# A hybrid mLSTM and SSD layer on one core: scalar and vector work queued behind the products' evacuations, with earlier first loads and other buffers for small rows

## The chip, the cores and the metric

The kernel runs on one core of one Trainium2 chip. The metric is the device time of one launch in microseconds; the time before is the median of three runs. A core has five engines with an instruction stream each, all in order: PE multiplies matrices into PSUM, DVE (vector) and ACT (scalar) read PSUM and SBUF, POOL works on SBUF, and SP issues the DMAs here. An instruction that waits holds up whatever stands behind it on its engine.

## The reference, cut to what matters

```python
h = rms_norm(x, norm_w)
proj = h @ w_in                                   # 2048 x 1024 times 1024 x 6680
q, k, v, i_pre, f_pre, o_pre, z_m, z_s, xbc, dt_raw = split(proj)
hm = mlstm_chunkwise(q, k, v, log_i, log_f)       # 4 heads, chunks of 128 tokens
hm = rms(hm) * mlstm_norm_w * sigmoid(o_pre) * silu(z_m)
xs, Bm, Cm = split(silu(causal_conv4(xbc)))
y = ssd_chunked(xs, dt, A, Bm, Cm) + d_skip * xs  # 2 groups of 8 heads, chunks of 128
y = grouped_rms(y * silu(z_s)) * ssd_norm_w
out = rms_norm(x + concat(hm, y) @ w_out, final_norm_w)
```

## The kernel before, in words

The sequence of 2048 tokens is worked in two halves (`s` = 0 and 1) and two output stages. Each of these four stages is a row of jobs: 26 jobs for each half (a pair of 128-column blocks of the input projection: for each head `h0` to `h3` four pairs, for each group `g0`, `g1` five) and eight jobs for each half of the output projection. A job is one Strassen product of 2x2 blocks with seven block products, each 12 matmuls of 128x128 by 128x512 (every operand is split into a high and a low part, three matmuls for each of four blocks). They all have line L270; the tile names tell the product: R11, R21, T2, T3, T1, R22, T4 are the right operands, L11, L12, S2, S3, S1, S4, L22 the left ones.

The seven right operands stay in SBUF for a stage. During the last job of a stage each is loaded anew for the next one (`refill`, L390, two 1 MB DMAs for each operand, high and low part). The left operands are made for each job from two weight (or mix) tiles by `left_sums` and `split` (L191 on ACT, L192 on DVE).

`strassen` accumulates four of the products in one PSUM tile `pa`, and copies an intermediate sum out after each: L276 after R11, L283 after T2, L289 after T1, and `copy` (L302 or L327) after R22. The next product into `pa` must wait for that copy. DVE adds two other tiles in (L280, L290, L296). Jobs overlap by two products, so that PE's order is T2, T3 of job n, R11 of job n+1, T1 of n, R21 of n+1, R22 of n, T4 of n. Between T1 and R22 stands only one other product.

After each product the function `step` runs. It first makes one piece of left operand (`left`), issues a refill if one is due, and then traces background work: gate computations and chunks that are due after so many steps (`tick`, `later`), generators planned for this step (`plan`), and one piece of the recurrence of the head or group whose projections were finished last (`wv.to`, class `Weave`). The background generators that matter here:

- `rec_head`: for each of eight chunks `load` (L676 `hin`, L678 the rows `nmi`), `scores` (L686 to L704: row mask on DVE, exponentials `E` L688 and `w` L690 on ACT, then matmuls L694), `memory` (L714 to L735), and later `turn`.
- `rec_group`: `load` (L788 `gin`), `decay` (L795 `E` loaded and made an exponential), `tokens` (matmuls L813, L814, L817), `states` (L841: four scalings of `y` on ACT), `update`, `outs`, and later `norm` (L889) and `spread` (L901).
- `next_h` and `next_w`: the right operands of the second half and of the output stages, made in the background and stored to DRAM. `next_w` loads four pieces of `w_out` (L532), scales them on ACT (L533), and `sums_out` forms the seven operands; each goes through two tiles of tag `hq` (three buffers), a high part made on ACT (L396) and a low part on DVE (L398), both stored by L537.

PE keeps the order in which the program is traced. On the other engines a planner sets the order when the program is built: among the instructions that its own model takes to be ready it places the first, so that background work can stand on ACT or DVE ahead of an evacuation that was traced before it. Buffers come from tags with a fixed number of slots; an instruction that needs a slot waits until the tile before has been used up.

Of the kernel before, what the change touches and what calls it, by code (L numbers as in the profile page):

```python
# [69 lines left out]
def hybrid_layer(ctx, tc, x, norm_w, w_in, b_igate, b_fgate, conv_w, conv_b, dt_bias,  # L70
# [35 lines left out]
    def r1(nm, n=NV):  # L106
        return mk([P, 272], "r1", 6, nm)[:, 0:n]

    def r5(nm, n=P):
        return mk([P, n], "r5", 9, nm)  # L110

# [153 lines left out]
    def product(ps, L, R, start):  # L265
        lh, ll = L
        rh, rl = R
        for k in range(4):
            for n, (l, r) in enumerate(((lh, rh), (lh, rl), (ll, rh))):
                nc.tensor.matmul(ps, lhsT=l[:, k, :], rhs=r[:, k, :], start=start and k + n == 0,  # L270
                                 stop=k == 3 and n == 2, skip_group_check=True)

    def strassen(L, R, oa, ob, copy):
        pa = pj_tile()
        product(pa, L["L11"], R["R11"], True)
        nc.scalar.copy(oa[0], pa)  # L276
        yield
        ps = pj_tile()
        product(ps, L["L12"], R["R21"], True)
        nc.vector.tensor_add(oa[0], ps, oa[0])  # L280
        yield
        product(pa, L["S2"], R["T2"], False)
        nc.scalar.copy(ob[0], pa)  # L283
        yield
        pd = pj_tile()
        product(pd, L["S3"], R["T3"], True)
        yield
        product(pa, L["S1"], R["T1"], False)
        nc.scalar.copy(ob[1], pa)  # L289
        nc.vector.tensor_add(ob[1], pd, ob[1])  # L290
        yield
        product(pa, L["S4"], R["R22"], False)
        copy(oa[1], pa)
        yield
        product(pd, L["L22"], R["T4"], False)
        nc.vector.tensor_add(ob[0], pd, ob[0])  # L296

# [3 lines left out]
    def evac_copy(dst, ps):  # L301
        nc.scalar.copy(dst, ps)  # L302

    def pair(L, R, s, ph, kind, j):
# [20 lines left out]
        if kind == "oz":  # L325
            def first(dst, ps):
                nc.scalar.activation(dst, ps, AF.Tanh, scale=0.5)  # L327

# [191 lines left out]
    def next_w():  # L520

        for j in range(2):
            for k in range(4):
                e = mk([P, HPG, P], "e4", 1, "we").rearrange("p a b -> p (a b)")
                q = {(0, 0): e[:, 0:TB], (1, 0): e[:, TB:]}
                for b in range(2):
                    q[b, 1] = mk([P, 6, P], "g3", 2, "wg").rearrange("p a b -> p (a b)")[:, 0:TB]
                for a in range(2):
                    r = j * 8 + a * 4 + k
                    for b in range(2):  # L530
                        u = q[a, b]
                        nc.sync.dma_start(u, w_out[r * P:(r + 1) * P, b * TB:(b + 1) * TB])  # L532
                        nc.scalar.activation(u, u, AF.Copy, scale=nwo[:, r:r + 1])  # L533
                yield

                def dst(o, i, v):
                    nc.sync.dma_start(wsd[j][o][:, i, k, :], v)  # L537

                yield from sums_out(q, dst)
# [128 lines left out]
    def rec_head(s, h):  # L668
# [3 lines left out]
        def load(n):  # L672
            b, c = seq[n]
            o = (b % 2) * TB + c * P
            t = r2("hin").rearrange("p (a l) -> p a l", a=4)
            nc.sync.dma_start(t, hd[s][h][:, 0:4, o:o + P])  # L676
            nmi = r2("nmi", 2 * P).rearrange("p (a l) -> p a l", a=2)
            nc.sync.dma_start(nmi, mrowd[b][:, h, c * P:(c + 1) * P].partition_broadcast(P))  # L678
            L["in", n] = (t, nmi)
# [27 lines left out]
        def memory(n):  # L707
# [11 lines left out]
            if C is None:  # L719
                C = S["C"] = mk([P, NV + 14], "C", 1, "C")[:, 0:NV]  # L720
                nc.vector.tensor_copy(C, cps[:, 0:NV])
# [8 lines left out]
            sq = mk([P, 1], "sq", 3, "sq")  # L730
            nc.scalar.activation(mk([P, DV], "r5", 9, "sj", BF16), nps[:, 0:DV], AF.Square, accum_out=sq)  # L731
            nc.scalar.copy(mx, nps[:, 0:DV])
# [21 lines left out]

        load(0)
        S["C"] = None
        if s:
            C = S["C"] = mk([P, NV + 14], "C", 1, "C")[:, 0:NV]
            nc.sync.dma_start(C, cd[h])
# [17 lines left out]
    def rec_group(s, g):  # L777
# [127 lines left out]
        load(0)  # L905
        decay(0)
        S["H"] = None
        if s:
# [25 lines left out]

    NREC = {"h": 10, "g": 25}

    class Weave:
# [3 lines left out]
        def set(self, g, n, total):  # L941
            self.finish()
            self.g, self.n, self.done, self.i, self.total = g, n, 1, 0, total
            next(g)
# [60 lines left out]
    def step(n, o):  # L1005

        left()
        if n + 1 < len(jobs) and jobs[n + 1]["new"]:
            st = jobs[n + 1]["stage"]
            Rs[st][o] = refill(o, refs[st])  # L1010
        tick()
        for t in [k for k in plan if k <= clock[0]]:
# [21 lines left out]
    for n, jb in enumerate(jobs):  # L1034
# [35 lines left out]
        if more:  # L1070
            next(jobs[n + 1]["gen"])
            step(n + 1, "R21")
        next(g)
        step(n, "R22")
        next(g)
        step(n, "T4")
        next(g, None)
        if "s" in jb and (n + 1 == len(jobs) or jobs[n + 1].get("ph") != jb["ph"]):
            nxt = [k for k in jobs[n + 1:] if k.get("ph") == jobs[n + 1].get("ph") and k["stage"] == jobs[n + 1]["stage"]]
            wv.set(rec(jb["s"], jb["ph"]), NREC[jb["ph"][0]], 7 * len(nxt) if "s" in jobs[n + 1] else 42)  # L1080
            if jb["ph"] == "h1":
                bgq = next_w() if jb["s"] else next_h()
                total = 64 if jb["s"] else 84
                for i in range(total):
# [31 lines left out]
```

## Time and profile before

| what | value |
|---|---|
| time, median of 3 runs (lowest to highest) | 1823.45 us (1819.24 to 1826.52) |
| time of the profiled execution | 1829.99 us |
| its span, first to last instruction | 1828.2 us |
| PE busy, weight load | 1679.5 us (92%), 1357.2 us (74%) |
| DVE, ACT, POOL busy | 1308.7 us (72%), 880.6 us (48%), 450.2 us (25%) |
| DMA moved, mean rate | 405.32 MB, 222 GB/s |
| mean granted TensorE clock | 0.966 of full speed |

PE is busy nearly all the time, so the span is PE's work, plus the stretches in which PE waits, plus what a lowered clock adds. Busy shares of the other engines do not bound the time by themselves; what counts is which of them PE waits for, and what stood ahead of the awaited instruction on its engine.

### The profile page before, as it was taken

The page shows a single profiled execution, that of the slowest core. Times are in us where ns is not written, and L with a number is a line of the kernel's source. Part 1 is how long each engine was busy: PE and PEld are TensorE (multiplying, and loading weights), DVE is VectorE, ACT ScalarE, POOL GpSimd, SP SyncE. Part 2 cuts the span into 40 slices and gives each one's busy share as a digit, 9 for nine tenths or more (in the row PEclk, how much of TensorE's full clock was granted, in tenths as well). Part 3 has the DMA queues.
Part 4 walks back from the last instruction along what each step waited for, and adds up shares of the span by engine and source line. Part 5 has one row for each costly group of instructions (what it writes and reads, how often), then busy time and mean ns, then how long its engine had stood idle before and what let it go on. Part 6 is the DMA issues. An engine that isn't in the chain of part 4 may idle for free.

```text
span 1828.2 us, 25057 instructions
## 1 busy us (share of the span) xinstructions
PE 1679.5 (92%) x8072; PEld 1357.2 (74%) x8072; DVE 1308.7 (72%) x2417; ACT 880.6 (48%) x1880; POOL 450.2 (25%) x629
## 2 busy tenths in 40 slices
PE   4999999999899798989899999898988889997997
PEld 4688887778788685767788777777776667776885
DVE  7677968877567693888675895655678578864775
ACT  5344644456566663434564444655565433332443
POOL 2000413332122131223121331202211144532222
PEclk9999999999999899999999999999999989998999
DMA  5245666668787689655575658888877976678543
GB/s 153 93 156 174 185 212 203 207 212 256 224 258 231 181 274 379 206 182 179 161 203 185 196 181 272 290 278 263 258 260 250 384 260 212 205 265 315 189 158 115
DMA packets 358323, 405.32 MB, mean 222 GB/s; under 512 B 30224, under 2 KB 284432, under 8 KB 352816
## 3 DMA queue, kind: packets, MB, share of 16 engines
q1 hardware_dynamic: 358192, 403.72, 68.1%
q8 instruction: 64, 1.05, 0.2%
q14 instruction: 67, 0.55, 0.1%
HBM read 251.40 MB, written 152.24 MB: 221 GB/s over the span
## 4 chain that ended last, share of the span: by engine, by line
PE 25%; DMA 15%; DVE 7%; issue 3%; ACT 2%; SPq 1%; POOL 1%; DVEq 0%; POOLq 0%; ACTq 0%
PE pj L270 21%; DMA E<-arow 1%; DMA we<-in_w_out 1%; DVE E L798 1%; DMA nmi<-mrow 1%; DMA mx<-mix 1%; DMA gin<-gd 1%; DMA ws1R<-hqh 1%; DMA T4l<-ws1T 1%; DMA ws0T<-hql 1%; DMA ws0R<-hqh 1%; DMA ws0T<-hqh 1%; DMA xr<-in_x 1%; DMA ws1T<-hqh 1%; PE rc L872 1%
## 5 line engine op out<-in xcount | busy, mean ns | idle before, releaser
L733 POOL TENSOR_SCALAR sq<-dn,sq 128x1 f32<-128x1 f32 x64 | 46.1, 720 | 624.9 <-ACT sj L731 477.8
L270 PE MATMUL pj<-R22h,S4h 128*128 128x512 f32 x272 | 119.7, 440 | 38.1 <-ACT ob L289 24.6
L270 PE MATMUL pj<-T2h,S2h 128*128 128x512 f32 x272 | 113.4, 417 | 11.6 <-ACT ca L276 9.3
L270 PE MATMUL pj<-T1l,S1h 128*128 128x512 f32 x272 | 107.3, 395 | 7.6 <-DMA T1l<-ws1T 7.2
L270 PE MATMUL pj<-R22l,S4h 128*128 128x512 f32 x272 | 113.1, 416 | 0.0
L270 PE MATMUL pj<-T4h,L22h 128*128 128x512 f32 x272 | 111.5, 410 | 1.4 <-DMA T4h<-ws1T 1.4
L270 PE MATMUL pj<-R11h,L11h 128*128 128x512 f32 x272 | 112.7, 414 | 0.0
L270 PE MATMUL pj<-R22h,S4l 128*128 128x512 f32 x272 | 112.7, 414 | 0.0
L270 PE MATMUL pj<-T2l,S2h 128*128 128x512 f32 x272 | 109.0, 401 | 4.0 <-DMA T2l<-hsT 3.3
L270 PE MATMUL pj<-T1h,S1h 128*128 128x512 f32 x272 | 111.0, 408 | 1.4 <-ACT cbt L283 1.4
L270 PE MATMUL pj<-R21h,L12h 128*128 128x512 f32 x272 | 110.1, 405 | 0.0
L270 PE MATMUL pj<-T3h,S3h 128*128 128x512 f32 x272 | 109.3, 402 | 0.0
L270 PE MATMUL pj<-T2h,S2l 128*128 128x512 f32 x272 | 108.6, 399 | 0.0
L270 PE MATMUL pj<-T1h,S1l 128*128 128x512 f32 x272 | 107.2, 394 | 1.3 <-DVE S1l L192 1.3
L270 PE MATMUL pj<-T4l,L22h 128*128 128x512 f32 x272 | 106.6, 392 | 1.9 <-DMA T4l<-ws1T 1.9
L270 PE MATMUL pj<-T4h,L22l 128*128 128x512 f32 x272 | 106.7, 392 | 0.0
L270 PE MATMUL pj<-R11h,L11l 128*128 128x512 f32 x272 | 106.6, 392 | 0.0
L270 PE MATMUL pj<-R11l,L11h 128*128 128x512 f32 x272 | 106.5, 391 | 0.0
L270 PE MATMUL pj<-T3h,S3l 128*128 128x512 f32 x272 | 106.3, 391 | 0.0
L270 PE MATMUL pj<-R21l,L12h 128*128 128x512 f32 x272 | 106.3, 391 | 0.0
L270 PE MATMUL pj<-R21h,L12l 128*128 128x512 f32 x272 | 106.3, 391 | 0.0
L270 PE MATMUL pj<-T3l,S3h 128*128 128x512 f32 x272 | 106.3, 391 | 0.0
(330 smaller groups left out, 4697.4 us busy)
## 6 DMA issues: line engine op xcount, KB each, us to landing
wa<-in_w_in SPq DMA_DIRECT2D x52, 512.0 KB, 6.2
s<-sum SPq DMA_DIRECT2D x52, 512.0 KB, 5.3
hd<-ob SPq DMA_DIRECT2D x32, 512.0 KB, 3.8
E<-arow SPq DMA_DIRECT2D x32, 512.0 KB, 5.2
hin<-hd SPq DMA_DIRECT2D x64, 256.0 KB, 4.7
mx<-mix SPq DMA_DIRECT2D x32, 512.0 KB, 4.9
wb<-in_w_in SPq DMA_DIRECT2D x26, 512.0 KB, 4.2
sum<-ls SPq DMA_DIRECT2D x26, 512.0 KB, 4.6
```

Source lines behind the costliest of these rows:

```text
L270: nc.tensor.matmul(ps, lhsT=l[:, k, :], rhs=r[:, k, :], start=start and k + n == 0, stop=k == 3 and n == 2, skip_group_check=True)
L733: nc.gpsimd.tensor_scalar(sq, dn, DV * EPS, sq, op0=ALU.mult, op1=ALU.add)
L798: nc.vector.tensor_scalar(E[:, r, :], E[:, r, :], G["cum"][:, c, k:k + 1], 0.0, op0=ALU.subtract, op1=ALU.min)
L872: nc.tensor.matmul(yps[o:o + HD, (r // 2) * P:(r // 2 + 1) * P], lhsT=xdt[:, r * HD:(r + 1) * HD], rhs=E[:, r, :], start=True, stop=True, ...
```

## The change

Four edits are made together.

1. Every evacuating instruction of `strassen` is recorded (`tie`): the last one on ACT under "a", the last on DVE under "v". In `step` all background work (`tick`, `plan`, `wv.to`, now in `behind`) is traced inside `tc.issue_after` of both: what it puts on ACT is placed behind the last recorded ACT instruction, what it puts on DVE behind the last DVE one. `left` and `refill`, the work at a job's end (tanh, convolution, stores) and the queues of POOL and SP are not tied.
2. The first piece of a recurrence (`load(0)`, and `decay(0)` for a group) is traced two products earlier, before R22 of the last job of its phase. A yield is added behind it, so the weave counts 11 pieces for a head and 26 for a group, of which two are done when it starts.
3. `next_w` loads its four pieces, yields three times, and only then scales them. Its pieces rise from 64 to 80 over the same 76 steps.
4. Buffers: the rows `nmi` move from tag `r2` (7 slots of 512 columns) to `r1`, which grows from 6 to 8 slots of 272 columns; `r5` shrinks from 9 to 8 slots of 128; the head state `C` takes the single slot of the group state `H`.

```diff
-        return mk([P, 272], "r1", 6, nm)[:, 0:n]
+        return mk([P, 272], "r1", 8, nm)[:, 0:n]
-        return mk([P, n], "r5", 9, nm)
+        return mk([P, n], "r5", 8, nm)
...
+    tied = {}
+
+    def tie(k, i):
+        tied[k] = i.ins
+
     def strassen(L, R, oa, ob, copy):
         pa = pj_tile()
         product(pa, L["L11"], R["R11"], True)
-        nc.scalar.copy(oa[0], pa)
+        tie("a", nc.scalar.copy(oa[0], pa))
...
-        nc.vector.tensor_add(oa[0], ps, oa[0])
+        tie("v", nc.vector.tensor_add(oa[0], ps, oa[0]))
...
         product(pa, L["S1"], R["T1"], False)
-        nc.scalar.copy(ob[1], pa)
-        nc.vector.tensor_add(ob[1], pd, ob[1])
+        tie("a", nc.scalar.copy(ob[1], pa))
+        tie("v", nc.vector.tensor_add(ob[1], pd, ob[1]))
...
                         nc.sync.dma_start(u, w_out[r * P:(r + 1) * P, b * TB:(b + 1) * TB])
-                        nc.scalar.activation(u, u, AF.Copy, scale=nwo[:, r:r + 1])
-                yield
+                for _ in range(3):
+                    yield
+                for a in range(2):
+                    r = j * 8 + a * 4 + k
+                    for b in range(2):
+                        nc.scalar.activation(q[a, b], q[a, b], AF.Copy, scale=nwo[:, r:r + 1])
...
-            nmi = r2("nmi", 2 * P).rearrange("p (a l) -> p a l", a=2)
+            nmi = r1("nmi", 2 * P).rearrange("p (a l) -> p a l", a=2)
...
-                C = S["C"] = mk([P, NV + 14], "C", 1, "C")[:, 0:NV]
+                C = S["C"] = mk([P, GW], "H", 1, "C")[:, 0:NV]
...
         load(0)
+        yield
         S["C"] = None
...
-    NREC = {"h": 10, "g": 25}
+    NREC = {"h": 11, "g": 26}
...
-            self.g, self.n, self.done, self.i, self.total = g, n, 1, 0, total
+            self.g, self.n, self.done, self.i, self.total = g, n, 2, 0, total
...
+        with ExitStack() as es:
+            for i in tied.values():
+                es.enter_context(tc.issue_after(i))
+            behind()
+
+    def behind():
         tick()
...
+        ends = "s" in jb and (not more or jobs[n + 1].get("ph") != jb["ph"])
+        if ends:
+            pre = rec(jb["s"], jb["ph"])
+            next(pre)
         next(g)
         step(n, "R22")
...
-            wv.set(rec(jb["s"], jb["ph"]), NREC[jb["ph"][0]], 7 * len(nxt) if "s" in jobs[n + 1] else 42)
+            wv.set(pre, NREC[jb["ph"][0]], 7 * len(nxt) if "s" in jobs[n + 1] else 42)
...
-                total = 64 if jb["s"] else 84
+                total = 80 if jb["s"] else 84
```

## Rows read from the trace of the kernel before

**Rows 1.** Waits of PE, whole span: line waited for, total us, times, longest us.

```profile
PE pj L270 <- ACT ob L289: 24.6, 10, 5.9
PE pj L270 <- ACT cbt L289: 13.4, 5, 5.4
PE rc L813 <- DMA gin<-gd: 12.0, 1, 12.0
PE pj L270 <- ACT ca L276: 9.3, 1, 9.3
PE rc L901 <- POOL dg L894: 4.1, 4, 1.7
```

**Rows 2.** Waits of ACT, whole span, in the same columns.

```profile
ACT w L690 <- DMA nmi<-mrow: 91.7, 36, 5.5
```

**Rows 3.** PE's timeline: start us, us, form, in brackets the idle time before.

```profile
899.57 0.79 PE L270 MATMUL pj<-R22h,S4h 128*128 128x512 f32 x1 [5.38 <-ACT cbt L289]
...
1168.55 0.80 PE L270 MATMUL pj<-R22h,S4h 128*128 128x512 f32 x1 [4.56 <-ACT ob L289]
...
1176.56 0.38 PE L694 MATMUL rc<-hin 128*128 128x128 f32 x2
...
1219.83 0.80 PE L270 MATMUL pj<-R22h,S4h 128*128 128x512 f32 x1 [4.37 <-ACT ob L289]
...
1276.39 0.79 PE L270 MATMUL pj<-R22h,S4h 128*128 128x512 f32 x1 [5.12 <-ACT ob L289]
...
1331.46 0.79 PE L270 MATMUL pj<-R22h,S4h 128*128 128x512 f32 x1 [4.45 <-ACT cbt L289]
```

**Rows 4.** ACT's timeline just before those copies, one leading wait for each.

```profile
897.17 0.29 ACT L690 ACTIVATE w<-nmi,u 128x1 f32<-128x1 f32 x1 [1.67 <-DMA nmi<-mrow]
...
1167.21 0.29 ACT L690 ACTIVATE w<-nmi,u 128x1 f32<-128x1 f32 x1 [3.77 <-DMA nmi<-mrow]
...
1216.84 0.72 ACT L533 ACTIVATE we<-we,nwo 128x512 f32<-128x512 f32 x1 [5.84 <-DMA we<-in_w_out]
...
1274.72 0.62 ACT L396 CAST hqh<-wg 128x512 fp32r<-128x512 f32 x1 [0.39 <-DMA ws1T<-hql]
...
1329.30 0.20 ACT L311 COPY cbt<-halo 128x3 f32<-128x3 f32 x1 [5.92 <-DMA hd<-ob]
```

**Rows 5.** The chain that ended last: start us, us, matmuls in the piece.

```profile
1168.55 5.21 PE pj L270 x12
1173.97 2.75 PE pj L270 x12
...
1469.41 7.49 PE pj L270 x24
```

**Rows 6.** Windows: length, busy of PE, PEld, DVE, ACT, POOL; granted clock, DMA share, GB/s.

```profile
1169.00:1173.00 4.00, 4.00 (x11) 3.03 (x11) 3.60 (x9) 2.82 (x8) 0.00 (x0) 0.50 0.85 281
1452.00:1474.00 22.00, 9.99 (x35) 8.04 (x34) 9.86 (x21) 4.85 (x9) 0.66 (x1) 0.69 1.01 370
```

**Rows 7.** SP's timeline at the change to the first output stage: issue time, us.

```profile
1447.39 0.32 SPq L261 DMA_DIRECT2D mx<-mix  x1
...
1451.98 0.59 SPq L390 DMA_DIRECT2D T4l<-ws0T  x1
1452.62 0.71 SPq L788 DMA_DIRECT2D gin<-gd  x1
...
1466.32 1.53 SPq L365 DMA_DIRECT2D xr<-in_x  x2
```

**Rows 8.** Waits of SP between 1440 and 1476 us.

```profile
SPq L365 <- DMA T4l<-ws0T: 1.2, 1, 1.2
```

**Rows 9.** Tile hqh, 1098 to 1400 us: who waited for it; its stores' time to landing.

```profile
DVE hql L398: 39.5, 27
...
DMA to landing us min/median/max: 2.0/4.1/7.5
```

**Rows 10.** Tile gin, whole span: duration ns min/median/max, first and last start us.

```profile
L841 ACT ACTIVATE y<-gin,dcol x128: 386/393/414, 273.0 to 1603.8; 128x128 f32<-128x128 f32 x128
```

More of the change, by code (lines that the diff above doesn't have):

```diff
@@ L279, in strassen @@
         product(ps, L["L12"], R["R21"], True)
-        nc.vector.tensor_add(oa[0], ps, oa[0])
+        tie("v", nc.vector.tensor_add(oa[0], ps, oa[0]))
         yield
         product(pa, L["S2"], R["T2"], False)
-        nc.scalar.copy(ob[0], pa)
+        tie("a", nc.scalar.copy(ob[0], pa))
         yield
@@ L288, in strassen @@
         product(pa, L["S1"], R["T1"], False)
-        nc.scalar.copy(ob[1], pa)
-        nc.vector.tensor_add(ob[1], pd, ob[1])
+        tie("a", nc.scalar.copy(ob[1], pa))
+        tie("v", nc.vector.tensor_add(ob[1], pd, ob[1]))
         yield
         product(pa, L["S4"], R["R22"], False)
-        copy(oa[1], pa)
+        tie("a", copy(oa[1], pa))
         yield
         product(pd, L["L22"], R["T4"], False)
-        nc.vector.tensor_add(ob[0], pd, ob[0])
+        tie("v", nc.vector.tensor_add(ob[0], pd, ob[0]))
     def halves(t, o=0):
@@ L301, in evac_copy @@
     def evac_copy(dst, ps):
-        nc.scalar.copy(dst, ps)
+        return nc.scalar.copy(dst, ps)
     def pair(L, R, s, ph, kind, j):
@@ L326, in first @@
             def first(dst, ps):
-                nc.scalar.activation(dst, ps, AF.Tanh, scale=0.5)
+                return nc.scalar.activation(dst, ps, AF.Tanh, scale=0.5)
             yield from strassen(L, R, halves(a), halves(b), first)
@@ L730, in memory @@
             sq = mk([P, 1], "sq", 3, "sq")
-            nc.scalar.activation(mk([P, DV], "r5", 9, "sj", BF16), nps[:, 0:DV], AF.Square, accum_out=sq)
+            nc.scalar.activation(mk([P, DV], "r5", 8, "sj", BF16), nps[:, 0:DV], AF.Square, accum_out=sq)
             nc.scalar.copy(mx, nps[:, 0:DV])
@@ L755, in rec_head @@
         load(0)
+        yield
         S["C"] = None
         if s:
-            C = S["C"] = mk([P, NV + 14], "C", 1, "C")[:, 0:NV]
+            C = S["C"] = mk([P, GW], "H", 1, "C")[:, 0:NV]
             nc.sync.dma_start(C, cd[h])
@@ L906, in rec_group @@
         decay(0)
+        yield
         S["H"] = None
@@ L1077, in hybrid_layer @@
         next(g, None)
-        if "s" in jb and (n + 1 == len(jobs) or jobs[n + 1].get("ph") != jb["ph"]):
+        if ends:
             nxt = [k for k in jobs[n + 1:] if k.get("ph") == jobs[n + 1].get("ph") and k["stage"] == jobs[n + 1]["stage"]]
-            wv.set(rec(jb["s"], jb["ph"]), NREC[jb["ph"][0]], 7 * len(nxt) if "s" in jobs[n + 1] else 42)
+            wv.set(pre, NREC[jb["ph"][0]], 7 * len(nxt) if "s" in jobs[n + 1] else 42)
             if jb["ph"] == "h1":
                 bgq = next_w() if jb["s"] else next_h()
-                total = 64 if jb["s"] else 84
+                total = 80 if jb["s"] else 84
                 for i in range(total):
```

## The prediction

> **What bounds the kernel now.** I read the waits of PE first, then PE's timeline at the longest of them, then ACT's timeline just before, then the chain at the same places, and last SP's timeline at the change of stage.
>
> PE runs without a stop except for a short list of waits. Two rows of it are the evacuation L289, the copy of the sum after T1 [rows 1]: 24.6 us in 10 waits and 13.4 in 5, so 38.0 us in 15. Next come 12.0 us for the first `gin` of a group, once, and 9.3 us for a copy L276, once. The matmuls that wait for L289 are R22h,S4h, since R22 accumulates into the tile that the copy reads and only one product stands between [rows 3]. The copy itself is short; what is late is its turn on ACT. At 1168.55 PE had waited 4.56 us [rows 3]. ACT had stood at L690, the `w` of a later chunk, until the rows `nmi` landed: 3.77 us idle, start at 1167.21 [rows 4]. The matmuls L694 of the same `scores` start at 1176.56 [rows 3], behind R22 and T4, so this `w` was traced after the copy and the planner had put it ahead of it. Over the whole span ACT waits 91.7 us in 36 places for `nmi` at L690 [rows 2]. Most of them hit no copy in its short gap, a few do. At 1219.83 the same happens with `we`, the first scaling of `next_w`: 5.84 us on ACT [rows 4], 4.37 on PE [rows 3].
>
> A wait costs more than its length. The twelve matmuls of R22 after the wait take 5.21 us, the next twelve 2.75 [rows 5]; the granted clock between 1169 and 1173 is 0.50, the lower of the two levels (1.2 of 2.4 GHz) [rows 6], after PE had stood still. So each of the long waits has 5.21 - 2.75 = 2.46 us behind it.
>
> **The tie.** It adds no instruction; it forbids ACT and DVE to begin background work of a step before that step's evacuation. Wait by wait:
>
> - 1168.55: `w` goes behind the copy, and behind R22's too. Whole wait and clock: 4.56 + 2.46 = 7.0 us.
> - 899.57, 5.38 us [rows 3]: ACT stood at a `w` again, but for 1.67 us of it [rows 4]; convolution work, which is not tied, stood beside it. Between 1.67 and 5.38 + 2.46 = 7.8; I take 4, the middle, as neither end is nearer.
> - 1276.39, 5.12 us [rows 3]: the last wait on ACT is 0.39 us at `hqh`, for a store of the tag `hq` [rows 4]. If that `hqh` was traced before the copy it stays ahead: 0. If behind: 5.12 + 2.46 = 7.6. I take 4.
> - 1331.46, 4.45 us [rows 3]: ACT stood 5.92 us at L311, a halo copy of a later convolution whose buffer was still being stored [rows 4]. That is work of a job's end, untied: 0.
> - The other ten waits at L289 hold 38.0 - (5.38 + 4.56 + 4.37 + 5.12 + 4.45) = 14.1 us. The longest is 5.9 [rows 1]; what stands before it is left-operand work, untied. For the small rest I take 2, between 0 and 8.
>
> What the tie adds is lateness: mask, exponentials and scalings that need no product of PE now start after it. Their readers are matmuls at least one piece of the weave later. For a head that is some eight microseconds away (R22 and T4 lie between the wait that ends at 1168.55 and the `scores` at 1176.56 [rows 3]), against four small instructions, `w` 0.3 us [rows 4]. I take 0 for heads. For a group the four scalings L841 move, 4 x 0.393 = 1.6 us for each of 32 chunks [rows 10]; they feed `y`, then POOL, then the matmuls L889 and L901, which already wait 4.1 us for POOL at L901 [rows 1]. Ends 0 and 1.6 x 32 = 50 us. I take 2, near the low end, since those matmuls are traced three and five steps after the chunk and wait four times in 64.
>
> **next_w.** At 1219.83 the loads get three yields, some three products of 2.75 us [rows 5], before ACT meets them, more than the 5.84 us waited [rows 4]: 4.37 + 2.46 = 6.8 us. The price: the seven pieces of `sums_out` for one unit now lie in 7/80 of 76 steps, 6.7, where they had 7/64, 8.3. Each piece takes two `hq` tiles of three. Stores land 4.1 us (median) to 7.5 after issue, and DVE's L398 already waits 39.5 us in 27 places for the high part or its slot [rows 9]. A fifth less time raises these waits; most fall into gaps of DVE. Ends 0 and 10 us of PE time (two more waits like 1276.39 with their clock, and some single microseconds); I take 3.
>
> **Earlier first loads.** The wait of 12.0 us for `gin` [rows 1] is at the change to the output stage. SP stands until 1447.39 for a mix tile, issues R22 and T4 of the refill, and `gin` only at 1452.62 [rows 7]. Two products earlier `gin` stands ahead of R22 and T4, and for this group the weave asks for it two steps later; that wait goes. What is late next: T4. Its low part landed at 1466.3, which SP's next issue waited for [rows 7, 8]. In the old run T4's product ends at 1469.41 + 7.49 = 1476.9 [rows 5]. In the new one it cannot start before T4l lands, so it ends at 1466.3 + 2.75 = 1469.1 at best: at most 7.9 us are won of the 12.0, and nothing of the clock's cost beside it. `gin`, `E` and the two `ea` are 384 + 512 + 256 KB by their shapes, 1.18 MB; the DMA engines are full here, share 1.01 at 370 GB/s [rows 6], so putting all of it ahead would delay T4 by 1.18 MB / 370 GB/s = 3.2 us. With a product at the low clock, 5.21 instead of 2.75, the gain falls to 2. Ends 2 and 8, I take 5.
>
> What this row shows is that whatever SP issues first lands first here. The Trainium skill, "DMA: Bandwidth & Descriptors", section Queues, rings and completion order, says that each DMA engine takes the descriptors of one issuing queue in ring order; that speaks against counting the 12.0 us whole, and by it alone the 3.2 us fall due in full, 4.7 instead of 5. The trace agrees: T4l, issued just before `gin`, landed just before it.
>
> The waits at the start and the tail are not touched.
>
> **Buffers.** `hin` has seven slots for itself, `nmi` shares eight with `vt`, `mx` and `g`. By the code a head holds three `nmi`, one or two `vt`, two `mx`, two `g`: eight or nine. At nine a load waits for one chunk's end, and it has three chunks' time to land. `r5` one fewer touches the gates' nine tiles, which are not live together. `C` and `H` never live together, as a weave ends before the next begins. Nothing, between -2 and +4 us; SP's stream is where a slot wait would show.
>
> **The sum.** Gains: 7.0 + 4 + 4 + 2 + 6.8 + 5 = 28.8 us. Costs: 2 + 3 = 5. Net 24 us from the profiled execution's 1829.99, which is 6.5 over the median; against the median of 1823.45 that is 1799.5, so 1800. With all gains at their lower ends (7.0 + 1.7 + 0 + 0 + 6.8 + 2 = 17.5) and costs of 10 + 4, 1820; with gains at the upper ends (7.0 + 7.8 + 7.6 + 8 + 6.8 + 8 = 45.2) and costs of 0, 1778.
>
> **Rivals.**
>
> - *The whole class goes.* ACT is freed of most of its 91.7 us, and the untied waits (1331.46 with 4.45, the one of 5.9, each with 2.46) shift out of the gap too: 15 us more, 1785, and with the copy L276 (9.3 us [rows 1]) 1775. For it: a freed ACT does left-operand work earlier. Against: their leading rows are DMAs into slots, which the tie does not bring sooner.
> - *The wait changes its cause.* The copy stays late because untied work is planned into the place of `w` (L191, L311) or because `hqh` and `hql` wait for their slots. Then the three waits that I count most on (7.0, 6.8 and 4) give back about two thirds, 12 us, and `hq` costs its 10: gain 28.8 - 12 - 10 - 2 = 5, 1818. The tie that changes nothing, since what is planned ahead belongs to earlier steps, ends in the same place; the distance from 1167.21 to 1176.56 speaks against that.
> - *Slower.* The tie makes each group chunk late: L841 behind the copies, POOL behind them, and L889 and L901 with PE in order behind that. 1.6 us x 32 = 50 us at the full price, 1800 + 50 = 1850. It decides from about (24 + 2) / 32 = 0.8 us for each chunk. Against it: the four waits in 64 at L901. For it: such matmuls do wait already, so the slack isn't large everywhere.
>
> **How the numbers follow.** Forecast 1800, by itself 1778 to 1815: 0.52. The whole class: 0.16. Changed cause: 0.20. Slower: 0.12. A measurement of this kernel tells about 0.5% from no change, 9 us: faster is under 1814, slower over 1833. Faster takes the forecast nearly whole and the first rival, 0.67; same the second rival and the forecast's edge, 0.21; slower 0.12. The range reaches from 1773, just under the first rival's lower time, to 1832: what is outside is the slower case and the last part of the first rival, under 0.2.
>
> **What would show it.** Right: L289's rows in PE's waits fall from 38 us to 15 or less, ACT's `nmi` row from 91.7 to under 15, the 12.0 us at L813 is gone and a wait for T4 of some microseconds stands near there, and the granted clock's mean rises. Wrong in a step: `we` still ahead of a copy (three yields too few); `hqh` or L398 rows well over the 39.5 us (the price of the denser pieces); waits at L889, L901, L714 or L872 that grow by tens of microseconds (the slower rival). The forecast is wrong altogether if PE's waits sum to as much as before under other names.

## The result: 1 % slower

The changed kernel takes 1842.74 us (median of four, 1840.83 to 1846.28); the kernel before, run beside it, 1824.99 (1819.24 to 1827.18). The ratio is 1.0104 with an interval of 1.0075 to 1.0134. The forecast was 1800 with a range of 1773 to 1832. It was wrong in sign, and the result lies outside the range. All ratios below are to the kernel before on the same chip. Its median there lay between 1824.99 and 1839.01 us, so ratios are compared and not times. A trace shows one execution; the two that are compared below are 10.9 us apart, less than the 17.8 of the medians, so they account for the smaller figure.

The page of the changed kernel begins with the span and the busy time of each engine:

```profile
span 1839.1 us, 25147 instructions
...
PE 1690.6 (92%) x8072; PEld 1363.6 (74%) x8072; DVE 1310.1 (71%) x2417; ACT 875.3 (48%) x1880; POOL 442.9 (24%) x629
```

Before, the span was 1828.2 and PE's busy time 1679.5. So PE stood 1828.2 - 1679.5 = 148.7 us then, and 148.5 now. The idle time is the same, though its largest items have gone; the same 8072 matmuls have become 11.1 us longer. The mean granted clock went from 0.966 to 0.964. Behind this small step stands more than it seems: summed over the stretches at the lower level (granted clock 0.50; 21 of them before, 27 now), PE worked 85.6 us in them before and 104.4 now. Two matmuls shown below take 1.20 us at that level and 0.60 at the full one; so, as an estimate, half of the 18.8 us more, 9.4, is what the clock added to the 11.1.

The waits of PE, whole span (line waited for: us in total, times, longest us). In this part of the code the line numbers are 5 higher than before (L294 is the old L289, L281 the old L276), in the recurrence 9 or 10 higher:

```profile
PE rc L703 <- DVE C L732: 11.6, 4, 5.2
...
PE pj L270 <- ACT ob L294: 7.3, 5, 3.5
PE rc L911 <- POOL dg L904: 6.9, 3, 2.9
PE rc L723 <- ACT vt L713: 6.0, 1, 6.0
PE rc L899 <- POOL q L893: 5.5, 4, 3.4
PE pj L270 <- ACT ca L281: 3.9, 1, 3.9
PE pj L270 <- ACT cbt L294: 3.9, 1, 3.9
...
PE pj L270 <- DMA R22h<-ws0R: 3.1, 1, 3.1
...
PE pj L270 <- DMA R22l<-ws0R: 2.3, 1, 2.3
...
PE pj L270 <- DMA T4l<-ws1T: 1.9, 1, 1.9
```

The copies that the forecast counted on did come sooner: the 38.0 us at the old L289 [rows 1] are 7.3 + 3.9 = 11.2, the 9.3 us at L276 [rows 1] are 3.9, and the 12.0 us for `gin` [rows 1] are gone. ACT's row for `nmi` [rows 2] has fallen from 91.7 us to 0.7. The time came back at the recurrence's own matmuls. Over all groups, PE's idle time before the products (tile `pj`) fell from 67.3 to 40.0 us, and before the matmuls of the recurrence, the gates and the transposes (tile `rc`) it rose from 70.5 to 97.6. PE's groups of the changed kernel (matrices, shapes, count; busy us and mean ns; idle before them and what ended it):

```profile
L727 PE MATMUL rc<-vt,kw 128*128 128x258 f32 x128 | 41.6, 409 | 4.8 <-ACT qg L516 2.6 <-DVE g L761 2.2
L723 PE MATMUL rc<-vt,st 128*128 128x258 f32 x128 | 41.4, 406 | 10.4 <-ACT vt L713 6.0 <-issue 2.3 <-DVE wa L207 2.0
...
L867 PE MATMUL rc<-xw,bt 128*128 128x512 f32 x64 | 36.7, 656 | 6.8 <-ACT emj L665 3.8 <-DVE cbm L837 1.7 <-DVE y L912 1.3
...
L703 PE MATMUL rc<-hin 128*128 128x128 f32 x128 | 25.7, 283 | 13.0 <-DVE C L732 11.6 <-ACT vt L713 1.0 <-DMA hin<-hd 0.3
...
L899 PE MATMUL rc<-ones,q 128*128 128x1 f32 x64 | 9.7, 221 | 10.1 <-POOL q L893 5.5 <-DVE xdt L834 4.5
```

The same groups of the kernel before:

```profile
L718 PE MATMUL rc<-vt,kw 128*128 128x258 f32 x128 | 38.4, 382 | 0.2 <-ACT mx L732 0.2
L714 PE MATMUL rc<-vt,st 128*128 128x258 f32 x128 | 38.6, 383 | 0.7 <-DVE dn L726 0.7
```

Read the column after the second bar: 0.2 has become 4.8, 0.7 has become 10.4. With L694 (3.3 to 13.0), L857 (1.3 to 6.8), L889 (3.5 to 10.1) and L901 (4.2 to 6.9) the idle time before these six lines went from 13.2 to 52.0 us. That is 38.8 more, against 38.0 + 9.3 - 11.2 - 3.9 = 32.2 won at the copies and about 4 at `gin`. The largest single item is new: 11.6 us for `C`, DVE's update of the head state (L732). The first column after the bar tells the rest: the busy time of these matmuls rose too, by 3.2 and 2.8 us in the two pairs shown and by 8.7 in all six, with no instruction added.

One place shows what the new waits are like. Around 1360 us, ACT's timeline of the changed kernel (start us, us, instruction; in brackets the idle time before):

```profile
1350.13 0.58 ACT L288 COPY cbt<-pj 128x512 f32<-128x512 f32 x1
...
1350.91 0.28 ACT L699 ACTIVATE w<-nmi,u 128x1 f32<-128x1 f32 x1
...
1359.08 0.58 ACT L281 COPY ca<-pj 128x512 f32<-128x512 f32 x1 [2.78 <-DMA gd<-ca]
...
1362.25 1.06 ACT L324 ACTIVATE cbt<-cd 128x1024 f32<-128x1024 f32 x1 [1.07 <-DVE cd L322]
1363.21 0.35 ACT L709 ACTIVATE kw<-rc,w 128x128 f32<-128x128 f32 x1
1363.46 0.36 ACT L713 COPY vt<-rc 128x256 f32<-128x256 f32 x1
```

and PE's in the same stretch, then two windows behind that wait (busy of PE, PEld, DVE, ACT, POOL; granted clock, DMA share, GB/s):

```profile
1348.47 0.38 PE L703 MATMUL rc<-hin 128*128 128x128 f32 x2
...
1363.92 1.20 PE L723 MATMUL rc<-vt,st 128*128 128x258 f32 x2 [5.99 <-ACT vt L713]
...
1375.80 0.60 PE L723 MATMUL rc<-vt,st 128*128 128x258 f32 x2
```

```profile
1363.90:1366.00 2.10, 2.08 (x5) 1.73 (x6) 2.10 (x3) 2.09 (x5) 0.00 (x0) 0.50 0.93 249
1366.00:1372.00 6.00, 6.00 (x24) 4.84 (x24) 3.83 (x11) 1.99 (x4) 0.00 (x0) 0.87 0.95 304
```

PE waits 5.99 us for `vt`, a copy of what PE itself had made from 1348.47 on. ACT comes to `kw` and `vt` only behind the evacuation L281, which can't write `ca` before the store `gd<-ca` of its old content has landed (2.78 us), and behind a step of the convolution that stands for DVE (1.07 us). The tie does not ask for all of that. This piece of the recurrence is traced behind T3, so it is tied to L288 at 1350.13; that `kw` and `vt` came behind L281 too is the planner's order, and what moved it is not shown. (The `vt` of the same chunk starts 4.6 us after its scores in the kernel before, 8.4 in `rest_only`, which has no tie, 13.3 in `act_tie` and 15.0 here.) A place where the tie itself holds the awaited work is shown below, in `act_only`. After the wait the two matmuls take 1.20 us, where two of the same form take 0.60 at 1375.80: the granted clock is at its lower level (0.50, 1.2 of 2.4 GHz) after PE stood still.

Set against the kernel before by the start of each job's R22 product, the changed kernel is even until 300 us, 7 us behind at 467, 13 to 14 by 740, 21.6 at 809, 6 at 1168, 12.4 at 1195, level at 1469 (the output stage, where the wait for `gin` is gone), 7 behind again one job later, at 1495, and 10.9 behind from 1700 on. So the loss comes in many stages, and no single wait makes it.

### The profile page after: what moved, and what is told of

Read it like the earlier page. It is cut to its first block, busy times and chain, and to the rows that moved or that the text cites. A ratio compares the mean times of both kernels' runs of the same rounds, so it can differ in the third digit from the quotient of the medians.

```text
span 1839.1 us, 25147 instructions
## 1 busy us (share of the span) xinstructions
PE 1690.6 (92%) x8072; PEld 1363.6 (74%) x8072; DVE 1310.1 (71%) x2417; ACT 875.3 (48%) x1880; POOL 442.9 (24%) x629
## 4 chain that ended last, share of the span: by engine, by line
PE 45%; DMA 15%; DVE 10%; issue 4%; ACT 3%; POOL 2%; SPq 1%; DVEq 0%; POOLq 0%; ACTq 0%
PE pj L270 36%; DMA E<-arow 2%; DVE E L808 2%; DMA s<-sum 1%; PE rc L727 1%; PE rc L882 1%; PE rc L723 1%; DMA z<-gd 1%; DMA we<-in_w_out 1%; PE rc L725 1%; DMA ws1T<-hqh 1%; DMA T4l<-ws1T 1%; PE rc L867 1%; DVE E L839 1%; DMA T4l<-ws0T 1%
## 5 line engine op out<-in xcount | busy, mean ns | idle before, releaser
L742 POOL TENSOR_SCALAR sq<-dn,sq 128x1 f32<-128x1 f32 x64 | 32.0, 500 | 682.4 <-ACT sj L740 343.5
```

Source lines behind the costliest of these rows:

```text
L742: nc.gpsimd.tensor_scalar(sq, dn, DV * EPS, sq, op0=ALU.mult, op1=ALU.add)
```

## Experiments

Theory A: the tie moves the head of the queue. It frees the copies, and makes the recurrence wait behind them. Theory B (rival): the tie is good and the other parts (buffers, earlier loads with the changed pace, `next_w`) cost it. Theory C (rival, after the first runs): DVE is full at the costly places, and any new order costs there.

### The parts on their own and together

`tie_only` is the kernel before with the whole tie, `rest_only` the changed kernel without it:

```diff
-        with ExitStack() as es:
-            for i in tied.values():
-                es.enter_context(tc.issue_after(i))
-            behind()
+        behind()
```

> The kernel before with the tie alone: background work on ACT and DVE behind the last evacuation, no other edit. Theory A (the tie itself costs: the recurrence's vector and scalar work starts later, and PE now waits at the recurrence's matmuls L714, L694, L857, L889 in place of the evacuation L289): slower than before, 1830 to 1845 us, the waits at L289 down to some 12 us, those at the recurrence's matmuls up by 30 us or more. Theory B (the loss comes from the other edits: the weave two pieces on, fewer r5 slots, denser pieces of next_w): faster than before, near 1805 us, and no rise at the recurrence's matmuls.

> The changed kernel without the tie: earlier first loads, the three yields in next_w, and the buffers, with the background work placed freely again. Theory A: about as before or faster, 1808 to 1824 us, the 12.0 us at the first gin gone but some 8 us at R22 and T4 of that job in their place, the waits at L289 still 25 us or more. Theory B: slower than before, 1832 to 1845 us.

`tie_only` 1.0098 [1.0071, 1.0126]; `rest_only` 1.0167 [1.0110, 1.0224]. Each alone costs about as much as the whole change or more, so neither theory holds alone, and the two don't add (0.98 + 1.67 = 2.65 %, against 1.04). In `tie_only` the waits for the copies fall (the old L289 to 23.9 us, L276 to none), and the idle time before the heads' matmuls (the old L694, L714 and L718) rises from 4.2 us to 34.2; its two largest rows:

```profile
PE rc L719 <- ACT vt L709: 15.1, 3, 12.3
PE rc L699 <- DVE C L728: 12.9, 5, 3.6
```

So the tie by itself moves the waits to the heads. In `rest_only` that idle time is 20.9 us: the other parts make the heads wait too.

`act_tie` and `dve_tie` are the changed kernel with the tie for one engine only (the line of `act_tie`; `dve_tie` has "v" in it):

```diff
-            for i in tied.values():
+            for i in [v for k, v in tied.items() if k == "a"]:
```

> The changed kernel with only ACT's background work tied, DVE's free. If the cost of the tie is DVE's (row masks, decay differences and other work that needs no product now stands behind an addition and piles up with the rest), this run wins back most of it: 1808 to 1822 us, with the L289 waits still at some 12 us. If the cost is ACT's (exponentials and scalings late), it stays at 1838 to 1846 us.

> The changed kernel with only DVE's background work tied, ACT's free. If the cost of the tie is DVE's: 1838 to 1850 us, as slow as with both, and the L289 waits back at 25 us or more, since w and the exponentials stand ahead of the copies again. If the cost is ACT's: 1815 to 1828 us.

`act_tie` 1.0018 [0.9993, 1.0044]; `dve_tie` 1.0255 [1.0205, 1.0305]. On top of the other parts ACT's tie brings 1.5 % (1.0167 to 1.0018), and DVE's takes 0.9 % (1.0167 to 1.0255, and 1.0018 to 1.0104).

Then each part on the kernel before: `act_only` (ACT's tie as in `act_tie`), `bufs_only` (the line shown, `r1` from 6 to 8 slots, `r5` from 9 to 8, and `C` in the buffer of `H`), `early_only` (the line shown, a yield after the first loads, one more in NREC, and the first loads before R22 of a phase's last job) and `nextw_only` (three yields ahead of the scalings, and a total of 80 for 64):

```diff
-            nmi = r2("nmi", 2 * P).rearrange("p (a l) -> p a l", a=2)
+            nmi = r1("nmi", 2 * P).rearrange("p (a l) -> p a l", a=2)
...
-            self.g, self.n, self.done, self.i, self.total = g, n, 1, 0, total
+            self.g, self.n, self.done, self.i, self.total = g, n, 2, 0, total
...
+                for _ in range(3):
+                    yield
...
-                total = 64 if jb["s"] else 84
+                total = 80 if jb["s"] else 84
```

> The kernel before with ACT's background work alone tied, no other edit. On the changed kernel the tie of ACT took 1.49 percent off (ratio to before 1.0167 without any tie, 1.0018 with ACT's) and the tie of DVE added 0.9 (1.0104 with both, 1.0255 with DVE's alone). If the two ties act the same way on the kernel before: both gave 1.0098, so ACT's alone gives about 1.000 to 1.001, between 0.985 and 1.002; the L289 waits fall to 15 to 25 us. If ACT's tie only mends what the other edits break (nmi later): 1.000 to 1.01, and no fewer waits at the recurrence's matmuls than in tie_only.

> The kernel before with the new buffers alone (nmi in r1 with 8 slots, r5 with 8, C in H's slot). Theory buffers (nmi now waits for a slot that vt, mx or g hold, lands later, and ACT's w waits longer, 131 us in rest_only against 92): 1.010 to 1.018, ACT's nmi row at 120 us or more. Theory weave (the pieces shifted by two steps and packed closer) or theory next_w: 0.997 to 1.004, the nmi row near 92 us.

> The kernel before with the earlier first loads alone (first piece two products earlier, 11 and 26 pieces, two done). Theory weave: 1.008 to 1.018, with the loss in the jobs of h2 and h3 of the first half. Theory buffers: 0.994 to 1.000, the 12.0 us at gin replaced by some 8 us at R22 and T4.

> The kernel before with the three yields of next_w alone. It can change nothing before the second half's h2 (about 1093 us), and rest_only had lost 20 us of its 42 by then, so it carries half at most: theory next_w (denser pieces wait for hq slots) 1.005 to 1.010, with more than 39.5 us of waits at hqh and hql; otherwise 0.994 to 1.002, with the wait of 4.4 us behind we gone.

`act_only` 1.0051 [1.0030, 1.0071], `bufs_only` 1.0089 [1.0064, 1.0114], `early_only` 1.0103 [1.0073, 1.0133], `nextw_only` 1.0036 [1.0010, 1.0061]. All four are slower than the kernel before. The last three sum to 2.28 %, against 1.67 % together; the intervals leave it open whether these three add.

`act_only` has the 9.3 us wait of [rows 1] in another dress. Its waits of PE (here too the line numbers are 5 higher than before: L719 is the old L714):

```profile
PE pj L270 <- ACT cbt L294: 16.3, 5, 4.4
PE rc L719 <- ACT vt L709: 14.0, 3, 11.1
PE rc L818 <- DMA gin<-gd: 12.8, 1, 12.8
PE pj L270 <- ACT ob L294: 11.8, 6, 4.0
```

That wait of the kernel before, on PE's timeline, and ACT's row of the copy (start us, us, instruction; idle time before):

```profile
631.11 0.80 PE L270 MATMUL pj<-T2h,S2h 128*128 128x512 f32 x1 [9.33 <-ACT ca L276]
```

```profile
630.48 0.59 ACT L276 COPY ca<-pj 128x512 f32<-128x512 f32 x1 [3.41 <-DMA gd<-ca]
```

ACT and PE of `act_only` at that place, with the scores of the chunk that PE then waits for:

```profile
629.33 0.58 ACT L281 COPY ca<-pj 128x512 f32<-128x512 f32 x1 [1.41 <-DMA gd<-ca]
629.81 0.40 ACT L693 ACTIVATE E<-E,lns 128x128 f32<-128x128 f32 x1
630.12 0.47 ACT L695 ACTIVATE w<-nmi,u 128x1 f32<-128x1 f32 x2
...
631.43 0.36 ACT L709 COPY vt<-rc 128x256 f32<-128x256 f32 x1
```

```profile
609.62 0.38 PE L699 MATMUL rc<-hin 128*128 128x128 f32 x2
...
631.89 1.20 PE L719 MATMUL rc<-vt,st 128*128 128x258 f32 x2 [11.06 <-ACT vt L709]
```

The copy stands for the store `gd<-ca` in both. Before, the next product's matmuls waited 9.33 us for the copy. Now the recurrence's matmuls wait 11.06 us for `vt`, queued behind the same copy. Here the tie itself does it: the scores at 609.62 are traced behind R11, so their `w` is tied to R11's evacuation and starts at 630.12, behind the copy at 629.33, and `kw` needs `w`. In the kernel before, the `w` of this chunk had started at 604.95. The tie changed who waits there, and not what for.

### Tying less

`w_tie` is the kernel before with one instruction tied, the `w` that waits for `nmi`; `dma_tie` ties beside it the others on ACT that waited for a DMA (`hqh`, the scalings of `next_w`, `ea`):

```diff
-            nc.scalar.activation(w, nmi[:, 0, P - 1:P], AF.Exp, bias=G["u"][:, c, h:h + 1])
+            with tc.issue_after(tied["a"]):
+                nc.scalar.activation(w, nmi[:, 0, P - 1:P], AF.Exp, bias=G["u"][:, c, h:h + 1])
```

> The kernel before with one instruction of each head chunk tied: w (L690 of before), the one that waits 92 us for nmi, goes behind the last copy on ACT; all other background work stays free. Theory bound (where a wait at a copy goes, vector work that is full there gives it back at the next matmul that needs it): 0.996 to 1.004, L289 down to some 28 us and the recurrence's matmuls up by as much. Theory lateness (the full tie only costs because exponentials and scalings other than w are late): 0.985 to 0.994, L289 down and no rise elsewhere.

> w_tie with the other ACT instructions that stand at a DMA or at a slot tied as well: hqh (L396 of before), the scalings of next_w (L533) and the group's second exponential ea. If what is wrong is only ACT standing at transfers ahead of a copy: 0.988 to 0.995, L289's waits under 20 us. If each further tie moves the waits on, as the full tie did: 0.996 to 1.004, with L289 lower and the recurrence's matmuls higher than in w_tie.

`w_tie` 0.9962 [0.9937, 0.9987]; `dma_tie` 0.9965 [0.9948, 0.9982]. These are the only versions here, with `bufs_wtie` below, whose interval lies under 1. So `w` alone carries the gain, and the other three bring nothing more that can be measured. Even in `w_tie` the store at 631 us keeps its price (waits of PE; the traced execution took 0.6 % more than the median):

```profile
PE pj L270 <- ACT ob L294: 20.7, 10, 5.8
...
PE rc L720 <- ACT vt L710: 11.9, 3, 10.7
PE pj L270 <- ACT cbt L294: 11.7, 4, 3.7
```

The copies wait 20.7 + 11.7 = 32.4 us, against 38.0 before [rows 1] and 11.2 in the changed kernel. The length of those waits doesn't order the ties: `w_tie` with 32.4 us and `dma_tie` with 27.9 are equally fast, `act_only` with 28.1 and `tie_only` with 23.9 are slower. It was the wrong quantity to minimise by itself.

### Buffers

`bufs_r1_10` gives `nmi`'s new tag ten slots (from `r2`, 7 to 6); `bufs_wtie` is `bufs_only` with the tie of `w`:

```diff
-        return mk([P, 272], "r1", 8, nm)[:, 0:n]
+        return mk([P, 272], "r1", 10, nm)[:, 0:n]
```

> bufs_only with r1 at 10 slots and r2 at 6: nmi always finds a slot, and hin has one less. Theory slots (bufs_only is 1.0089 because nmi waits for a slot and lands just when w stands at the head of ACT, 134 us against 92): the nmi row falls to 95 us or less, 0.998 to 1.003. If the nmi row stays at 120 us or more, it is not the slots but where the planner puts w: 1.006 to 1.012.

> bufs_only (1.0089) with w tied behind the last copy on ACT (w_tie without the buffers was 0.9962). If the buffers cost through ACT standing at w for nmi: 0.995 to 1.000, the nmi row gone. If they cost by other slots (r5 with 8, C in H's slot, hin loaded ahead of others): 1.003 to 1.009.

`bufs_r1_10` 1.0208 [1.0182, 1.0234]; `bufs_wtie` 0.9978 [0.9957, 0.9998]. ACT's largest wait in `bufs_only`:

```profile
ACT w L690 <- DMA nmi<-mrow: 134.1, 46, 5.3
```

That is the row of [rows 2], which was 91.7 in 36 waits; with ten slots it is still 131.7, so it isn't a shortage of slots in `r1`. (The time of `bufs_r1_10` lies above both of the ranges that were expected; whether the slot taken from `r2` makes it was not tested.) With `w` tied the row is gone and so is the loss, from 1.0089 to 0.9978. So the new homes cost through `w`: it stood at the head of ACT's queue more often and longer. Why it did is not shown.

### Pace of the weave

`early_oldpace` is `early_only` with the pieces at their old steps:

```diff
-            while self.g is not None and self.done < self.n and self.done * (self.total - 3) < i * self.n:
+            while self.g is not None and self.done < self.n and (self.done - 1) * (self.total - 3) < i * (self.n - 1):
```

> The kernel before with the earlier first loads, but the pieces behind them at the steps they had in the kernel before (the weave counts from the second piece). Theory pace (early_only is 1.0103 because the pieces start two steps later and stand closer): 0.994 to 1.000, the 12.0 us at gin replaced by some 8 us, no rise at L718, L889 and L857. Theory load (the early load itself collides with slots or transfers): 1.006 to 1.013.

1.0026 [1.0011, 1.0041], against 1.0103. Of what the earlier loads cost, 0.8 % is the pace: counting the first loads as a done piece makes a head's next piece start two steps later and the others stand closer. The loads themselves cost about 0.3 % (0.1 to 0.4 by the interval).

### DVE and the controls

`before_taps` and `act_taps` leave out two of the convolution's three added taps, the kernel before and `act_only`; that takes vector work away from the costly places:

```diff
-                for q in range(1, 4):
+                for q in range(1, 2):
```

> The kernel before with two of the three vector steps of the convolution left out (taps 2 and 3), so that DVE has 48 instructions of 1.2 us less, all in the convolution's jobs. Theory bound (DVE is full where these jobs lie, and the wait of 9.3 us for a copy L276 at 631 us stems from it): 0.975 to 0.99, that wait gone. Theory chain (PE's waits come from order and transfers, not from DVE's load): 0.995 to 1.000.

> act_only with the same two taps left out. Theory bound: ACT's tie now pays, at least 0.5 percent under before_taps (act_only was 0.5 percent over the kernel before), and the wait of 11.1 us at the first recurrence matmul of that place is gone. Theory chain: 0.3 to 0.7 percent over before_taps, the waits at the recurrence's matmuls as in act_only.

`before_taps` 0.9986 [0.9963, 1.0010], `act_taps` 1.0012 [0.9987, 1.0037]. With the vector work cut ACT's tie still costs 0.26 % by the medians, where it cost 0.51; the intervals overlap, so a part may go with DVE's load: the wait for `vt` at 631 us is 8.20 us in `act_taps`, 11.06 in `act_only`. Taking that work out doesn't make the kernel before measurably faster, though, and ACT's tie gains nothing from it. That speaks against theory C as the main cause; its share in DVE's tie was not tried.

`after_free` is the changed kernel with the DVE operations that need no product (mask, `qp`, the decay differences) exempt from the tie:

```diff
-            nc.vector.scalar_tensor_tensor(E, nmi[:, 0, :], G["u"][:, c, h:h + 1], maskneg,
-                                           op0=ALU.add, op1=ALU.min)
+            free.add(nc.vector.scalar_tensor_tensor(E, nmi[:, 0, :], G["u"][:, c, h:h + 1], maskneg,
+                                                    op0=ALU.add, op1=ALU.min).ins.name)
```

> The changed kernel with both ties, but the vector work that needs no product exempt from DVE's: the row mask, qp and a group chunk's eight decay differences. Theory lateness (DVE's tie costs because this work leaves the gaps before an addition and piles up behind it): back at the level of act_tie, 1.000 to 1.005. Theory order (tying the work that reads the products' neighbours in PSUM costs as well): 1.008 to 1.012, as the changed kernel.

1.0100 [1.0062, 1.0138], no different from the 1.0104 of the whole change. So the lateness of these operations isn't the main part of what DVE's tie costs.

`shift_bg` moves the operands' background by one step and nothing else, to see what a new order costs by itself:

```diff
-                    at(3 + i * 76 // total, bgq)
+                    at(4 + i * 76 // total, bgq)
```

> A control: the kernel before with the background operands of the second half and the output (next_h, next_w) one step later, nothing else. No mechanism costs or gains more than 3 us here. If any new placing by the planner costs by itself (the order before being a fortunate one): 1.003 to 1.010. If the edits cost by their own mechanisms alone: 0.998 to 1.002.

1.0016 [0.9995, 1.0038]: no difference that can be measured. The losses of 0.5 to 1 % above are more than a mere shuffle gave here; it is one shuffle only.

### The change mended

`after_mended` keeps buffers, earlier loads and `next_w`, ties `w` alone, and keeps the old pace:

```diff
+            with tc.issue_after(tied["a"]):
+                nc.scalar.activation(w, nmi[:, 0, P - 1:P], AF.Exp, bias=G["u"][:, c, h:h + 1])
...
-            while self.g is not None and self.done < self.n and self.done * (self.total - 3) < i * self.n:
+            while self.g is not None and self.done < self.n and (self.done - 1) * (self.total - 3) < i * (self.n - 1):
...
-            for i in tied.values():
-                es.enter_context(tc.issue_after(i))
-            behind()
+        behind()
```

> The changed kernel with w alone tied in place of all background work, and the pieces of the weave at the steps of the kernel before: buffers, next_w and early loads stay. If the buffers cost only through w (bufs_wtie 0.9978 against w_tie 0.9962) and the early loads through their pace (1.0026 with the old pace against 1.0103): 0.996 to 1.004, at least 0.6 percent under the changed kernel's 1.0104. If the parts cost by themselves whatever ACT does: 1.006 to 1.012.

1.0015 [0.9999, 1.0031], 0.9 % under the whole change. The width of the tie and the pace together hold nearly all of the loss. The other parts bring nothing over `w_tie`, which stays, with `dma_tie`, the fastest kernel here.

## Why the prediction was wrong, step by step

**Right: the diagnosis and the awaited waits.** ACT did stand at `w` ahead of copies, and putting `w` behind them is worth 0.4 % by itself (`w_tie`). The signs named for it came as said: the old L289's waits at 11.2 us (15 or less was expected), `nmi` at 0.7 (under 15), no wait for `gin`.

**Right: `gin`.** Forecast were 5 us of the 12.0. SP of the changed kernel at the change of stage, issue times:

```profile
1458.72 0.43 SPq L798 DMA_DIRECT2D gin<-gd  x1
...
1459.84 0.38 SPq L395 DMA_DIRECT2D R22h<-ws0R  x1
...
1465.64 0.32 SPq L395 DMA_DIRECT2D T4l<-ws0T  x1
```

`gin` now goes ahead of R22 and T4 [rows 7], and the waits for these two are 3.1 + 2.3 + 0.7 + 1.9 = 8.0 us: some 4 us are left of the 12.0. The Trainium skill ("DMA: Bandwidth & Descriptors", Queues, rings and completion order) says that each DMA engine takes a queue's descriptors in ring order; this trace agrees in that the wait went from `gin` to the operands issued behind it.

**Wrong: "What the tie adds is lateness ... I take 0 for heads."** This is the first step that failed. Between issue and reader I had counted some eight microseconds and four small instructions, and had taken the copy itself as ready. The tie puts the head's work behind a copy that can wait too, for a buffer's store (629.33 in `act_only`), and `w`, `kw` and `vt` are then late by that whole wait and the queue behind it. The heads' matmuls (the old L694, L714 and L718) waited 24.0 us more in the changed kernel, 28.2 against 4.2, in place of 0, and 30.0 more with the tie alone. The tied orders differ in which heads wait: the 11.06 us at 631 us is `act_only`'s, the 5.99 at 1363.92, whose cause is open, the changed kernel's. On DVE the same happens to `C`. The longest of its waits is 5.17 us before L703 at 1196.97, for a `C` whose product PE had finished near 1185; DVE's timeline there:

```profile
1185.20 0.69 DVE L403 TENSOR_TENSOR hql<-wg,hqh 128x512 fp32r<-128x512 f32 x1 [4.67 <-DMA ws0T<-hqh]
...
1187.48 0.68 DVE L301 TENSOR_TENSOR ob<-pj,ob 128x512 f32<-128x512 f32 x1
...
1194.23 0.69 DVE L403 TENSOR_TENSOR hql<-we,hqh 128x512 fp32r<-128x512 f32 x1 [3.40 <-DMA ws0R<-hqh]
...
1196.44 0.48 DVE L732 SCALAR_TENSOR_TENSOR C<-C,nmi,rc 128x258 f32<-128x258 f32 x1
```

DVE stands twice for stores of `hq`. The tie holds `C` behind L301; what stands after that is the planner's order. L703's wait for `C` is 0 in the kernel before and in `rest_only`, 3.7 us in `early_only`, and 4.2 to 13.3 in `act_only`, `act_tie`, `tie_only` and `dve_tie`.

In the forecast's own terms: the tie stood in the sum at 7.0 + 4 + 4 + 2 - 2 = 15 us won, and `tie_only` lost 0.98 %, some 18 us. The other parts stood at 6.8 - 3 + 5 = 8.8 us won, and `rest_only` lost 1.67 %, some 30 us. Both halves were wrong in sign, so the steps that follow count as much as this one.

**Wrong in size: groups.** 2 us were taken, between 0 and 50. The idle time before the old L889 and L901 rose by 6.6 + 2.7 = 9.3, and before L857 by 5.5. Of the 9.3, 5.4 us are waits for POOL, where the slower rival looked for them; whether the scalings L841 made POOL late was not traced. At its decisive rate of 0.8 us for each of 32 chunks it would have been 26. So it is not the cause by itself.

**Wrong: the clock counted on one side only.** To the long waits at evacuations I added 2.46 us of slow matmuls, and to none of the waits that a tie might bring. PE's busy time rose by 11.1 us, where it should have fallen; some 9.4 of it is the clock, by the estimate above. The sign that the mean granted clock rises did not come (0.966, then 0.964).

**Wrong: next_w.** The wait at 1219.83 was to go with three yields. In the kernel before with `next_w` alone it is still there, ACT and then PE:

```profile
1217.18 0.72 ACT L538 ACTIVATE we<-we,nwo 128x512 f32<-128x512 f32 x1 [7.01 <-DMA we<-in_w_out]
```

```profile
1218.94 0.79 PE L270 MATMUL pj<-R22h,S4h 128*128 128x512 f32 x1 [4.50 <-ACT ob L289]
```

The planner put the scaling ahead of the copy again, so a later place in the trace of the program didn't make it later on ACT (over the span ACT waits 15.3 us for `we`, 11.4 before). The 6.8 us never came (`nextw_only` 1.0036). In the changed kernel `we` is tied, and PE waits 3.52 us at the same product, since left-operand work, which is not tied, stands for its DMA ahead of that copy: the wait changed its cause, as the second rival has it. The waits at `hqh` [rows 9] rose from 39.5 to 50.7 us, the sign named for the denser pieces, but these don't make it: `nextw_only` has 32.7 us, and `tie_only`, with the old pieces, 66.8. It is a cost of the tie that the sum did not have.

**Wrong: "Buffers ... Nothing".** I counted slots, and in `r1` slots were not short. With the new homes `w` stood longer (134.1 us, 1.0089), for a reason that is not shown. Under the tie of the changed kernel that row is gone; on the kernel before it was the dearest part but one.

**Not costed: the pace.** I saw the two steps of delay for `gin` alone, and took the edit to `done` as keeping time. It is worth 0.8 % of the kernel (`early_only` against `early_oldpace`).

**Foreseen only as a sentence.** "The forecast is wrong altogether if PE's waits sum to as much as before under other names" is what happened, 148.7 and 148.5 us. It stood under the signs and had no chance. Of the rivals, *the wait changes its cause* (1818) is nearest in mechanism, but kept a net gain; *slower* (1850, 0.12) is nearest in time, but blamed the groups alone.

**Open.** What DVE's tie costs, 0.5 to 0.9 %, is not settled. With it DVE waits longer for products: in `dve_tie`

```profile
DVE ob L301 <- PE pj L270: 50.0, 25, 6.8
```

where the kernel before has 28.9 us; the changed kernel has 46.7, but `act_tie`, without that tie, has 39.6 already. `after_free` rules out the operations without a product as the main part; whether those with one or the background of the operands make it wasn't told apart. Why the tie and the other parts don't add (2.65 against 1.04 %) is open too, and whether the store at 631 us could land earlier wasn't tried.

## What to carry to other kernels

When an engine in order stands for one late input ahead of urgent work, move that one instruction behind the urgent work, and leave the rest: tying `w` alone gave -0.4 %, tying all of ACT's background work +0.5 %, tying DVE's as well +1.0 %. Before you count a wait as won, ask what the urgent instruction itself may wait for, since all that you queue behind it inherits that wait; and price the clock for waits that come as you do for waits that go. Cost a pacing formula like any other edit: shifting when pieces start cost more here than the loads that it came with.
